# Gate chunks by twos: the seven products in another order, and a fourth place for split halves in the last pair

## The chip, the cores and the metric

The kernel runs on one core of a Trainium2 chip. The metric is the device time of one execution in microseconds (us); lower is better. Three runs of the kernel before were timed, and one further execution was profiled.

## The reference, cut to what is computed

One layer of a hybrid encoder trunk on 256 tokens of 2048 features: a mixer of two branches (retention and a gated delta rule), cross-attention, an MLP. Only the mixer's gates matter here:

```
proj = h @ w_in            # rg, gz, gate_a, gate_b are four of its parts, 2048 columns each
yr = silu(rg) * yr         # retention's output and its swish gate
yg = silu(gz) * yg         # the delta rule's output and its gate
merged = sigmoid(gate_a) * yr + sigmoid(gate_b) * yg
out = merged @ w_out
```

All data are float32. The products are computed to float32 accuracy from halves: a value is split into a rounded high half and the rest, and three matmuls (high x high, high x low, low x high) make one product.

## The kernel before

The mixer goes over four groups of columns `j` = 0 to 3, in each of which retention, the delta rule's stream and both branches' gates are computed. h1, the normalised input, stands as four quads of 512 features (each a high and a low half, 4 tiles of 128 features x 256 tokens). A gate chunk is 512 columns of `w_in`: 2048 x 512 weights in four quarters, one to a quad, of 1 MiB each. A quarter is loaded as `raw` by a DMA of SyncE's queue (SP) and split in two steps of 128 x 1024: ScalarE (ACT) copies the high half `whi` (L990), VectorE (DVE) subtracts and leaves the low half `wlo` (L991). The pool has three places for such a pair of halves, so the fourth split waits for the matmuls that read the first. A `spare` pool gives a fourth place (`whx`, `wlx`) to every fourth split; only the MLP uses it.

Retention's gate chunks of j = 1, 2, 3 and the delta rule's of j = 3 are computed by twos, in `two_chunks`. Two chunks are two columns of blocks, `n` = 0 and 1, over the quads `q`, and the two token tiles `t` of 128 are the rows. Two of the four quads are computed plainly: `plain(n, q)` is 24 matmuls (4 feature tiles x 2 token tiles x 3). For the two other quads, 2 x 2 blocks of tokens and features meet 2 x 2 blocks of weights, and seven products do the work of eight: b11, p5, b22, the second sum of x, b21, y and the fourth sum of x. A product is 12 matmuls. It needs sums of tokens (`s_in`, built once by `sums_of_tokens` when j = 1, L936) and sums of weights, x and y, each in two tiles (`xa`, `xb`, `ya`, `yb`) of 128 x 1024. A sum of weights is built by a plain load through SP's queue (`load_parts`) and an adding transfer through GpSimd's (POOL) queue (`add_parts`, L971, 512 KB each), or by an addition on VectorE (`add_to`, L977). x changes its value three times in a pair, each time by a transfer that adds to what is there, so it cannot start before the last split that reads the old value. `moved` says which sums go by transfers.

`finish` adds the kept sums (`u`, `d`) to a chunk's result and applies the gate: `gth` (L1087, L1089), then a product with `yr` or `yg`. `others(q)` is used in the last pair alone: `take_back(q)` splits a kept quad `mg` of merged results of an earlier j again, by a copy q (L1128) and a subtraction (L1129), into a quad of h1 that no one reads any more. It is the operand of `w_out`, which follows the last pair. In the retention pairs steps of the delta rule's core (`steps`, with `ro` at L274 on GpSimd, `qe` at L855 and `yg` at L858) stand between the products: `step` runs one after each product and after every four triples (12 matmuls) of a plain product.

Every engine runs its own queue in order. The order comes from the order of the program and from priorities: loads, splits and adding transfers run ahead of the matmuls that need them (`tc.high_priority`), `tc.issue_after` keeps chosen instructions of one engine in sequence, and `behind` puts work behind the latest split.

Of the kernel before, what the change touches and what calls it, by code (L numbers as in the profile page):

```python
# [10 lines left out]
F32 = mybir.dt.float32  # L11
# [6 lines left out]
P = 128  # L18
# [36 lines left out]
def trunk(ctx: ExitStack, tc: tile.TileContext, x_f, mem_f, positions, lead_f, small_f, w_blocks, w_chunks, w_ga,  # L55
# [30 lines left out]
    def half_tiles():  # L86

        turn[0] += 1
        if spare and turn[0] % 4 == 0:
            return tuple(spare[0].tile([P, 1024 + room], F32R, name=nm, tag=nm, bufs=1)  # L90
                         for nm, room in (("whx", 128), ("wlx", 0)))
        return tuple(wp.tile([P, 1024 + room], F32R, name=nm, tag=nm, bufs=3) for nm, room in (("whi", 64), ("wlo", 0)))

    @contextmanager
# [841 lines left out]
    def sums_of_tokens(i):  # L936

        xs = mx.tile([P, 2, 512], F32, name="xs", tag="qk", bufs=1)
        whole, sv = (xs[:, e, :].rearrange("p (a n) -> p a n", a=n) for e, n in ((0, 2), (1, 4)))
        for g in range(2):  # L940
            vec.tensor_add(whole[:, g], *(h1[g].both[:, i, c:c + S].bitcast(F32) for c in (0, S)))
        (a11, a21), (a12, a22) = ((whole[:, g, 0:P], whole[:, g, P:S]) for g in range(2))
        vec.tensor_sub(sv[:, 0], a21, a22)
        vec.tensor_sub(sv[:, 1], sv[:, 0], a11)
        vec.tensor_sub(sv[:, 2], a11, a21)
        vec.tensor_add(sv[:, 3], a12, sv[:, 1])
        split([a[:, i, :] for a in s_in], xs[:, 1, :])

    def two_chunks(chunks, evacs, before=None, moved=("x2", "x4", "y")):

        own = [stream_ps(), stream_ps()]
        shared, p5 = bank("c"), bank("c")
        kept_back.append(None)
        x, y = ([mx.tile([P, 1024], F32, name=n, tag=tag, bufs=1) for n, tag in these]
                for these in ((("xa", "kq"), ("xb", "lw")), (("ya", "qk"), ("yb", "tw"))))
        opened, ends = set(), []

        def lines(n, q, h):  # L960
            return w_chunks[chunks[n], q][:, h * 1024:(h + 1) * 1024]

        def load_parts(to, n, q):
            with tc.high_priority(offset=100000), tc.issue_after(fetched[-1]):
                for h in range(2):
                    fetched.append(nc.sync.dma_start(to[h], lines(n, q, h)).ins)

        def add_parts(to, n, q):
            with tc.high_priority(offset=100000):
                for h in range(2):  # L970
                    pool.dma_start(to[h], lines(n, q, h), accum_op=ALU.add)  # L971

        def add_to(to, src):
            with tc.high_priority(offset=100000):
                for h in range(2):
                    with tc.issue_after(latest["lo"]):
                        vec.tensor_add(to[h], to[h], src[h])  # L977

        def load(n, q):
            raw = wp.tile([P, 4 * 512], F32, name="raw", tag="raw", bufs=3)  # L980
            with tc.high_priority(offset=100000):
                fetched.append(nc.sync.dma_start(raw, w_chunks[chunks[n], q]).ins)
            return raw[:, 0:1024], raw[:, 1024:2048]

        def parted(srcs):
            halves = []
            with tc.high_priority(offset=100000):
                for src in srcs:
                    hi, lo = (h[:, :1024] for h in half_tiles())
                    latest["hi"] = act.activation(hi, src, AF.Copy).ins  # L990
                    latest["lo"] = vec.tensor_sub(lo, src, hi.bitcast(F32)).ins  # L991
                    halves.append([a.rearrange("p (k n) -> p k n", n=512) for a in (hi, lo)])
            return halves

        def triple(o, lhs, rhs, key):
            for l, r in ((0, 0), (0, 1), (1, 0)):
                with tc.issue_after(ends[-1]) if ends else ExitStack():
                    ins = pe.matmul(o, lhs[l], rhs[r], start=key not in opened, stop=False, skip_group_check=True).ins  # L998
                opened.add(key)
            return ins  # L1000

        def product(o, lhs, srcs, key):
            halves = parted(srcs)
            for i in range(4):
                ins = triple(o, lhs(i), [a[:, i % 2, :] for a in halves[i // 2]], key)
            ends.append(ins)
            step()

        def plain(n, q, by_rows=False):
            halves = parted(load(n, q))  # L1010
            for c, (i, t) in enumerate([(i, t) for t in range(NT) for i in range(4)] if by_rows else
                                       [(i, t) for i in range(4) for t in range(NT)]):
                ins = triple(own[n][t], [a[:, i, t * P:(t + 1) * P] for a in h1[q]],
                             [a[:, i % 2, :] for a in halves[i // 2]], (n, t))
                if c % 4 == 3:
                    ends.append(ins)
                    step()

        def part(g, t):
            return lambda i: [a[:, i, t * P:(t + 1) * P] for a in h1[g]]  # L1020

        def summed(c):
            return lambda i: [a[:, i, c * P:(c + 1) * P] for a in s_in]

        def kept_sum(tag, ps):
            o = mx.tile([P, 2, 512], F32, name="u", tag=tag, bufs=1)
            act.activation(o[:, 0], ps, AF.Copy)
            return o

        def finish(n, t, more):  # L1030
            with tc.high_priority(offset=50000):
                evacs[n](t, own[n][t], 0, 512, more)

        def others(q):
            if before:
                before(q)

        plain(0, 2)
        load_parts(x, 1, 0)
        if "x1" in moved:  # L1040
            add_parts(x, 0, 0)
        b11 = load(0, 0)
        product(shared, part(0, 0), b11, "shared")
        if "x1" not in moved:
            add_to(x, b11)
        with tc.high_priority(offset=50000):
            u = kept_sum("vh", shared)
        u1, u3 = u[:, 0], u[:, 1]
        product(p5, summed(0), x, "p5")
        add_parts(x, 1, 1)  # L1050
        plain(0, 3)
        load_parts(y, 1, 0)
        if "y" in moved:
            add_parts(y, 1, 1)
        b22 = load(1, 1)
        product(own[1][0], summed(3), b22, (1, 0))
        product(shared, summed(1), x, "shared")
        add_parts(x, 0, 1)
        if "y" not in moved:
            add_to(y, b22)  # L1060
        with tc.high_priority(offset=50000):
            d = kept_sum("vl", shared)
        others(1)
        plain(1, 2)
        b21 = load(0, 1)
        product(own[0][0], part(1, 0), b21, (0, 0))
        finish(0, 0, u1)
        product(shared, summed(2), y, "shared")
        with tc.high_priority(offset=50000):
            act.activation(u3, shared, AF.Copy)  # L1070
            vec.tensor_sub(d[:, 0], p5, d[:, 0])
            vec.tensor_sub(d[:, 1], p5, u3)
        product(own[0][1], part(1, 1), x, (0, 1))
        finish(0, 1, u3)
        others(2)
        with behind():
            others(3)
        plain(1, 3, True)
        kept_back.clear()
        for t in range(NT):  # L1080
            finish(1, t, d[:, t])

    def gates():
        def gate_of(ps, f, scale, more):
# [20 lines left out]

        def of_retention(j, yr):
            if j in (1, 2, 3):
                two_chunks((H_RG + j, H_TA + j), (silu_gate(yr), sig_gate(yr)))
                return
            chunk(h1, cols(w_chunks, H_RG + j), silu_gate(yr))  # L1110
            chunk(h1, cols(w_chunks, H_TA + j), sig_gate(yr))

        def of_delta_rule(j, yr, yg, quad, before=None):
            if j in (3,):
                two_chunks((H_GZ + j, H_TB + j), (silu_gate(yg), sig_gate(yg, yr)), before, ("x1", "x2", "x4"))
            else:
                chunk(h1, cols(w_chunks, H_GZ + j), silu_gate(yg))
                chunk(h1, cols(w_chunks, H_TB + j), sig_gate(yg, yr), before=before, cuts=2 if before else 1)
            to_feature(lambda t, f: yg[:, t, f * P:(f + 1) * P], quad)
# [434 lines left out]
    for fb in range(4):  # L1554
# [4 lines left out]
        for b2 in range(8):  # L1559
# [13 lines left out]
            blocks(h3, w_ff1, 8 * fb + b2, 2, evac_h, ends)  # L1573
            if fb == 0:
                if b2 == 0:
                    spare.append(fp)
                for b8 in ((), (0, 1, 2), (3, 4, 5), (6, 7), (), (), (), ())[b2]:
                    place(b8)
            if b2 > 2:
# [72 lines left out]
```

## Time and profile before

| | |
|---|---|
| runs | 2036.26, 2037.98, 2039.83 us; median 2037.98 |
| profiled execution: own time, span | 2036.82 us, 2035.1 us |
| granted TensorE clock, mean | 0.999 |
| TensorE busy | 2020.7 us, 99% of the span |
| VectorE, ScalarE, GpSimd busy | 1618.4 us (80%), 1239.9 us (61%), 63.2 us (3%) |
| retention's pairs | 524 to 579, 739 to 793, 953 to 1008 us |
| the delta rule's pair | 1008 to 1056 us |

TensorE is busy nearly throughout, so what the change can move is TensorE's idle time and the number of its matmuls. In the profile a tile's name is given without its number; q is any quad (h1's or one taken back), `sh` and `sl` are the halves of `s_in`, `s` and `b` are PSUM banks, L998 is the one line that issues all matmuls of the pairs. A row of a timeline has the start, the time, the engine, the line, the operation and the tile, and in brackets how long the engine sat idle before and for whom. The rest of the profile is read in the prediction.

### The profile page before, as it was taken

Reading aid. Unit: us, or ns where it says so; the run is one execution under the profiler, and the core shown is the slowest. Engines: PE = TensorE matmul, PEld = TensorE weight load, DVE = VectorE, ACT = ScalarE, POOL = GpSimd, SP = SyncE. Lnnn points to the kernel's source line nnn. Section 1 sums busy time; section 2 is a strip of 40 time slices with the busy share of each in tenths; the row PEclk is TensorE's granted clock in tenths of the full one; section 3 lists DMA queues with packets and bytes.
Section 4 is the critical chain, followed back from the end, with each engine's and each line's share of the span. In section 5 each row is a group of like instructions: output and inputs, shape, how many; then the busy total and the mean of one; then the engine's idle time right before and its main releaser. Section 6 shows DMA issues by size and latency. Waiting matters only on the chain.

```text
span 2035.1 us, 28641 instructions
## 1 busy us (share of the span) xinstructions
PE 2020.7 (99%) x10742; PEld 1741.5 (86%) x10742; DVE 1618.4 (80%) x2507; ACT 1239.9 (61%) x2029; POOL 63.2 (3%) x74
## 2 busy tenths in 40 slices
PE   9999999999999999999999999999999999999998
PEld 8888888988888888888878899888888888888886
DVE  5887788879778887888877766777887887888788
ACT  5665765675567555755655565566557556656665
POOL 0000000000100010000100000000000000000000
PEclk9999999999999999999999999999999999999999
DMA  8678556455945585557876654568546646554661
GB/s 329 206 265 293 186 184 200 158 191 188 282 166 181 193 265 184 191 180 238 253 225 232 212 182 164 175 217 277 207 135 238 215 156 220 196 205 171 237 233 62
DMA packets 84683, 422.03 MB, mean 207 GB/s; under 512 B 17072, under 2 KB 25152, under 8 KB 40256
## 3 DMA queue, kind: packets, MB, share of 16 engines
q1 hardware_dynamic: 80656, 406.93, 57.7%
q0 software_dynamic: 3456, 12.58, 3.4%
q8 instruction: 84, 1.38, 0.3%
q10 hardware_dynamic: 432, 0.69, 0.1%
q14 instruction: 55, 0.45, 0.1%
HBM read 406.52 MB, written 11.55 MB: 205 GB/s over the span
## 4 chain that ended last, share of the span: by engine, by line
PE 96%; DVE 2%; DMA 1%; issue 0%; ACT 0%; POOLq 0%; DVEq 0%; POOL 0%; ACTq 0%
PE s L218 52%; PE s L1398 7%; PE b L1398 7%; PE s L998 5%; PE s L175 5%; PE s L174 5%; PE s L176 5%; PE b L998 2%; PE s L407 1%; PE s L408 1%; PE s L409 1%; PE b L802 1%; PE b L705 1%; PE b L146 1%; PE b L835 1%; PE b L145 1%
## 5 line engine op out<-in xcount | busy, mean ns | idle before, releaser
L218 PE MATMUL s<-q,whi 128*128 128x512 f32 x2824 | 971.0, 391 | 0.0
L129 ACT ACTIVATE whi<-raw 128x1024 fp32r<-128x1024 f32 x535 | 567.7, 1061 | 420.1 <-PE s L218 222.3
L130 DVE TENSOR_TENSOR wlo<-raw,whi 128x1024 fp32r<-128x1024 f32 x535 | 652.2, 1221 | 213.3 <-ACT whi L129 209.5
L218 PE MATMUL s<-q,wlo 128*128 128x256 f32 x2824 | 765.1, 281 | 0.0
L218 PEld LDWEIGHTS s<-q,whi 128*128 128x128 f32 x2824 | 521.5, 188 | 100.6
L218 PEld LDWEIGHTS s<-q,wlo 128*128 128x128 f32 x2824 | 528.5, 188 | 13.4 <-DVE wlo L130 0.4
L175 PE MATMUL s<-wlo,q 128*128 128x512 f32 x448 | 176.3, 394 | 0.0
L176 PE MATMUL s<-whi,q 128*128 128x512 f32 x448 | 174.6, 390 | 0.0
L174 PE MATMUL s<-whi,q 128*128 128x512 f32 x448 | 159.0, 390 | 0.0
L227 ACT ACTIVATE bo<-s 128x256 f32<-128x256 f32 x192 | 73.2, 381 | 109.9 <-PE s L218 109.8
L1398 PE MATMUL s<-whi,q 128*128 128x512 f32 x384 | 122.1, 389 | 0.0
L228 DVE TENSOR_TENSOR bo<-bo,s 128x256 f32<-128x256 f32 x192 | 79.9, 416 | 40.9 <-ACT bo L227 40.4
L998 PE MATMUL s<-whi,q 128*128 128x512 f32 x320 | 101.3, 390 | 0.0
L174 PEld LDWEIGHTS s<-whi,q 128*128 128x128 f32 x448 | 84.0, 188 | 17.5
L176 PEld LDWEIGHTS s<-whi,q 128*128 128x128 f32 x448 | 84.2, 188 | 16.8
L175 PEld LDWEIGHTS s<-wlo,q 128*128 128x128 f32 x448 | 84.2, 188 | 16.5
L1421 DVE TENSOR_TENSOR wlo<-rt,whi 128x1024 fp32r<-128x1024 f32 x55 | 67.4, 1225 | 35.9 <-ACT whi L1420 35.5
L218 PE MATMUL s<-q,whx 128*128 128x512 f32 x248 | 86.6, 390 | 0.0
L1398 PEld LDWEIGHTS s<-whi,q 128*128 128x128 f32 x384 | 72.1, 188 | 15.0
L1420 ACT ACTIVATE whi<-rt 128x1024 fp32r<-128x1024 f32 x55 | 58.3, 1061 | 41.7 <-PE s L1398 29.4
L991 DVE TENSOR_TENSOR wlo<-raw,whi 128x1024 fp32r<-128x1024 f32 x56 | 68.1, 1223 | 13.6 <-ACT whi L990 13.3
L990 ACT ACTIVATE whi<-raw 128x1024 fp32r<-128x1024 f32 x56 | 59.0, 1058 | 29.5 <-PE s L998 17.8
(405 smaller groups left out, 2977.0 us busy)
## 6 DMA issues: line engine op xcount, KB each, us to landing
raw<-w_ff SPq DMA_DIRECT2D x96, 1024.0 KB
raw<-w_chunks SPq DMA_DIRECT2D x76, 1024.0 KB
raw<-w_blocks SPq DMA_DIRECT2D x64, 1024.0 KB
raw<-w_xk SPq DMA_DIRECT2D x16, 1024.0 KB
raw<-w_out SPq DMA_DIRECT2D x16, 1024.0 KB
raw<-w_xq SPq DMA_DIRECT2D x16, 1024.0 KB
raw<-w_xo SPq DMA_DIRECT2D x16, 1024.0 KB
rt<-w_ff SPq DMA_DIRECT2D x16, 1024.0 KB
```

What stands on the lines that cost most here:

```text
L129: latest["hi"] = act.activation(hi[:, cs], src[:, cs], AF.Copy).ins
L130: latest["lo"] = vec.tensor_sub(lo[:, cs], src[:, cs], hi[:, cs].bitcast(F32)).ins
L174: pe.matmul(o, xh, wh, start=first, stop=False)
L175: pe.matmul(o, xh, wl, start=False, stop=False)
L176: pe.matmul(o, xl, wh, start=False, stop=last)
L218: ins = pe.matmul(ps[b][:, :S] if part else ps[b], halves[h][part][:, i, b * P:(b + 1) * P], x[:, kk % 4, :], start=kk == 0 and not part, ...
L227: act.activation(o, ps[b][:, S:], AF.Copy)
L228: vec.tensor_add(o, o, ps[b][:, :S])
L991: latest["lo"] = vec.tensor_sub(lo, src, hi.bitcast(F32)).ins
L998: ins = pe.matmul(o, lhs[l], rhs[r], start=key not in opened, stop=False, skip_group_check=True).ins
L1398: ins = pe.matmul(o, lhs[l], rhs[r], start=key not in opened, stop=last and j == 2, skip_group_check=True).ins
L1421: latest["lo"] = vec.tensor_sub(lo, raw[:, c:c + 1024], hi.bitcast(F32)).ins
```

## The change

The two chunks of a pair change places (the sigmoid's chunk is now `n` = 0), the plain products take quads 0 and 1, the seven products quads 2 and 3, and the order is another: `plain(1, 0)` stands before the second sum of x, and the product of x's fourth sum is the last of the pair, behind the last plain product and behind `finish` of chunk 1. In the last pair there is a fourth place for halves, in the tiles "kq" and "lw" that x had; x goes to "r4" and "g_a"; y is summed by adding transfers, and `take_back` no longer waits by `behind`.

```diff
     def half_tiles():
         turn[0] += 1
         if spare and turn[0] % 4 == 0:
-            return tuple(spare[0].tile([P, 1024 + room], F32R, name=nm, tag=nm, bufs=1)
-                         for nm, room in (("whx", 128), ("wlx", 0)))
+            return spare[0]()
...
     def sums_of_tokens(i):
-            vec.tensor_add(whole[:, g], *(h1[g].both[:, i, c:c + S].bitcast(F32) for c in (0, S)))
+            vec.tensor_add(whole[:, g], *(h1[2 + g].both[:, i, c:c + S].bitcast(F32) for c in (0, S)))
...
-    def two_chunks(chunks, evacs, before=None, moved=("x2", "x4", "y")):
+    def two_chunks(chunks, evacs, before=None, moved=("x2", "x4", "y"), places=("kq", "lw")):
-        own = [stream_ps(), stream_ps()]
+        own = {1: stream_ps(), 0: stream_ps()}
...
-        plain(0, 2)
-        load_parts(x, 1, 0)
+        plain(0, 0)
+        load_parts(x, 1, 2)
         if "x1" in moved:
-            add_parts(x, 0, 0)
-        b11 = load(0, 0)
-        product(shared, part(0, 0), b11, "shared")
+            add_parts(x, 0, 2)
+        b11 = load(0, 2)
+        product(shared, part(2, 0), b11, "shared")
...
         product(p5, summed(0), x, "p5")
-        add_parts(x, 1, 1)
-        plain(0, 3)
-        load_parts(y, 1, 0)
+        add_parts(x, 1, 3)
+        plain(0, 1)
+        load_parts(y, 1, 2)
         if "y" in moved:
-            add_parts(y, 1, 1)
-        b22 = load(1, 1)
+            add_parts(y, 1, 3)
+        b22 = load(1, 3)
         product(own[1][0], summed(3), b22, (1, 0))
+        others(1)
+        plain(1, 0)
         product(shared, summed(1), x, "shared")
-        add_parts(x, 0, 1)
+        add_parts(x, 0, 3)
...
-        others(1)
-        plain(1, 2)
-        b21 = load(0, 1)
-        product(own[0][0], part(1, 0), b21, (0, 0))
-        finish(0, 0, u1)
+        others(2)
+        b21 = load(0, 3)
+        product(own[0][0], part(3, 0), b21, (0, 0))
         product(shared, summed(2), y, "shared")
...
-        product(own[0][1], part(1, 1), x, (0, 1))
-        finish(0, 1, u3)
-        others(2)
-        with behind():
-            others(3)
-        plain(1, 3, True)
-        kept_back.clear()
+        plain(1, 1, True)
+        others(3)
         for t in range(NT):
             finish(1, t, d[:, t])
+        finish(0, 0, u1)
+        product(own[0][1], part(3, 1), x, (0, 1))
+        kept_back.clear()
+        finish(0, 1, u3)
...
-                two_chunks((H_RG + j, H_TA + j), (silu_gate(yr), sig_gate(yr)))
+                two_chunks((H_TA + j, H_RG + j), (sig_gate(yr), silu_gate(yr)))
...
-                two_chunks((H_GZ + j, H_TB + j), (silu_gate(yg), sig_gate(yg, yr)), before, ("x1", "x2", "x4"))
+                spare.append(lambda: tuple(mx.tile([P, 1024], F32R, name=nm, tag=tag, bufs=1)
+                                           for nm, tag in (("whx", "kq"), ("wlx", "lw"))))
+                two_chunks((H_TB + j, H_GZ + j), (sig_gate(yg, yr), silu_gate(yg)), before, ("x1", "x2", "x4", "y"), ("r4", "g_a"))
+                spare.clear()
```

Three places show how the change moves instructions. Line numbers of the changed kernel are one or two lower.

ScalarE in the last pair, around the product p5. raw_10028 is the load of b11, raw_10074 that of the plain product behind p5, raw_10110 (raw_10112 after) that of b22, and xa_9986, xb_9987 are x. Before:

```order
L990 ACTIVATE whi_10030<-raw_10028 128x1024
L990 ACTIVATE whi_10034<-raw_10028 128x1024
L1089 ACTIVATE gth_9975<-gth_9975 128x512
L990 ACTIVATE whi_10052<-xa_9986 128x1024
L990 ACTIVATE whi_10056<-xb_9987 128x1024
L990 ACTIVATE whi_10076<-raw_10074 128x1024
L1027 ACTIVATE u_10050<-b_9984 128x512
L1128 ACTIVATE q_10268<-mg_6710 128x4x256
L990 ACTIVATE whi_10080<-raw_10074 128x1024
L990 ACTIVATE whi_10112<-raw_10110 128x1024
```

and now:

```order
L989 ACTIVATE whi_10034<-raw_10028 128x1024
L989 ACTIVATE whi_10052<-xa_9986 128x1024
L1087 ACTIVATE gth_9951<-gth_9951 128x512
L989 ACTIVATE whi_10076<-raw_10074 128x1024
L1087 ACTIVATE gth_9975<-gth_9975 128x512
L989 ACTIVATE whi_10080<-raw_10074 128x1024
L1026 ACTIVATE u_10050<-b_9984 128x512
L1129 ACTIVATE q_10195<-mg_6710 128x4x256
L989 ACTIVATE whx_10056<-xb_9987 128x1024
L989 ACTIVATE whi_10114<-raw_10112 128x1024
```

The split of `xb`, which p5 reads, stood ahead of both splits of raw_10074; now it stands behind them and behind the copies u and q.

GpSimd's queue over the beginning of the last pair. Before:

```order
L274 TENSOR_TENSOR ro_9707<-qe_9705,nhalf_pow_89 128x4
L971 DMA xa_9986<-w_chunks 128x1024
L971 DMA xb_9987<-w_chunks 128x1024
L274 TENSOR_TENSOR ro_9707<-qe_9705,nhalf_pow_89 128x4
L971 DMA xa_9986<-w_chunks 128x1024
```

and now:

```order
L273 TENSOR_TENSOR ro_9707<-qe_9705,nhalf_pow_89 128x4
L970 DMA xa_9986<-w_chunks 128x1024
L273 TENSOR_TENSOR ro_9707<-qe_9705,nhalf_pow_89 128x4
L970 DMA ya_9988<-w_chunks 128x1024
L970 DMA yb_9989<-w_chunks 128x1024
L970 DMA xb_9987<-w_chunks 128x1024
L970 DMA xa_9986<-w_chunks 128x1024
```

Two adding transfers for y are new, and the first one for `xb` went behind them and behind a step of the core.

VectorE at the end of the second retention pair; raw_7880 is the load of the work that follows the pair, and q, yg, qe, ro belong to the delta rule's core. Before:

```order
L1087 TENSOR_TENSOR gth_7828<-s1_7445,u_7546 128x512
L855 SCALAR_TENSOR_TENSOR qe_7600<-so_7601,qe4_5769 128x4
L130 TENSOR_TENSOR wlo_7883<-raw_7880,whi_7882 128x1024
L1095 SCALAR_TENSOR_TENSOR yr_7013<-gth_7828,yr_7013 128x512
L858 SCALAR_TENSOR_TENSOR yg_7014<-b_7698,ro_7602,small_111 128x128 x4
L1087 TENSOR_TENSOR gth_7866<-s0_7446,u_7723 128x512
L130 TENSOR_TENSOR wlo_7887<-raw_7880,whi_7886 128x1024
```

and now:

```order
L1085 TENSOR_TENSOR gth_7838<-s0_7444,u_7757 128x512
L854 SCALAR_TENSOR_TENSOR qe_7600<-so_7601,qe4_5769 128x4
L1093 SCALAR_TENSOR_TENSOR yr_7013<-gth_7838,yr_7013 128x512
L857 SCALAR_TENSOR_TENSOR yg_7014<-b_7700,ro_7602,small_111 128x128 x4
L990 TENSOR_TENSOR wlo_7855<-xb_7451,whi_7854 128x1024
L1085 TENSOR_TENSOR gth_7842<-s1_7445,u_7757 128x512
L129 TENSOR_TENSOR wlo_7883<-raw_7880,whi_7882 128x1024
L129 TENSOR_TENSOR wlo_7887<-raw_7880,whi_7886 128x1024
```

The last product of the pair needs wlo_7855; its subtraction now stands behind the gate and the core's normalisation, and both subtractions of the following load stand behind it.

More of the change, by code (lines that the diff above doesn't have):

```diff
@@ L947, in sums_of_tokens @@
         split([a[:, i, :] for a in s_in], xs[:, 1, :])
-    def two_chunks(chunks, evacs, before=None, moved=("x2", "x4", "y")):
-        own = [stream_ps(), stream_ps()]
+    def two_chunks(chunks, evacs, before=None, moved=("x2", "x4", "y"), places=("kq", "lw")):
+        own = {1: stream_ps(), 0: stream_ps()}
         shared, p5 = bank("c"), bank("c")
         kept_back.append(None)
-        x, y = ([mx.tile([P, 1024], F32, name=n, tag=tag, bufs=1) for n, tag in these]
-                for these in ((("xa", "kq"), ("xb", "lw")), (("ya", "qk"), ("yb", "tw"))))
+        x, y = ([mx.tile([P, 1024], F32, name=n + e, tag=tag, bufs=1) for e, tag in zip("ab", tags)]
+                for n, tags in (("x", places), ("y", ("qk", "tw"))))
         opened, ends = set(), []
@@ L1575, in trunk @@
                 if b2 == 0:
-                    spare.append(fp)
+                    spare.append(lambda: tuple(fp.tile([P, 1024 + room], F32R, name=nm, tag=nm, bufs=1)
+                                               for nm, room in (("whx", 128), ("wlx", 0))))
                 for b8 in ((), (0, 1, 2), (3, 4, 5), (6, 7), (), (), (), ())[b2]:
```

## Prediction

> **What bounds the kernel now.** I read the page's busy shares first, then the waits of TensorE, then a table of the four stretches in which pairs of gate chunks are computed, and last, instruction by instruction, the places where TensorE stood still. The page's engine line and the whole list of TensorE's waits:
>
> ```profile
> PE 2020.7 (99%) x10742; PEld 1741.5 (86%) x10742; DVE 1618.4 (80%) x2507; ACT 1239.9 (61%) x2029; POOL 63.2 (3%) x74
> PE s L998 <- DVE wlo L991: 2.7, 3, 1.5
> PE b L266 <- DVE warm L262: 1.1, 1, 1.1
> PE s L407 <- DVE q L343: 1.1, 1, 1.1
> PE b L998 <- DVE wlo L991: 0.4, 1, 0.4
> ```
>
> TensorE is the bound for 99% of the span. Only the rows of L998, the matmuls of the pairs, touch what is changed; they add up to 3.1 us in four waits, each for a low half `wlo` that VectorE subtracts. Which pair has them shows in the stretches (after the colon: length; then busy time and instructions of PE, weight loads, VectorE, ScalarE, GpSimd; granted clock, DMA share, GB/s):
>
> ```profile
> 524.00:579.00 55.00, 55.00 (x294) 47.10 (x293) 45.98 (x73) 36.36 (x61) 10.76 (x12) 1.00 0.76 215
> 953.00:1008.00 55.00, 55.00 (x292) 47.06 (x291) 45.93 (x73) 35.26 (x59) 11.44 (x12) 1.00 0.86 243
> 1008.00:1056.00 48.00, 44.84 (x198) 35.61 (x197) 39.22 (x40) 29.98 (x34) 3.46 (x4) 1.00 0.74 235
> ```
>
> In the first and third retention pairs (the second, not shown, is alike) TensorE is busy in the whole stretch: a rearrangement there has nothing to win. All four waits lie in the last stretch, the delta rule's pair. TensorE's timeline at them, and the chain of waits ahead of the first two:
>
> ```profile
> 1028.02 0.50 PE L998 MATMUL b<-wlo,sh 128*128 128x512 f32 x1 [0.44 <-DVE wlo L991]
> 1029.29 0.61 PE L998 MATMUL s<-whi,q 128*128 128x512 f32 x2
> 1031.43 0.50 PE L998 MATMUL s<-wlo,q 128*128 128x512 f32 x1 [1.52 <-DVE wlo L991]
> 1031.76 0.40 PE L998 MATMUL s<-whi,q 128*128 128x512 f32 x1
> 1046.25 0.50 PE L998 MATMUL s<-wlo,q 128*128 128x512 f32 x1 [1.00 <-DVE wlo L991]
> 1048.58 0.50 PE L998 MATMUL s<-wlo,q 128*128 128x512 f32 x1 [0.20 <-DVE wlo L991]
> 1016.25 9.29 DMA xb<-w_chunks
> 1029.02 1.22 DVE yb L977
> 1030.24 1.15 DVE wlo L991
> 571.13 6.60 PE s L998 x29
> ```
>
> The last row, 29 matmuls of the first pair in 6.60 us, gives the pace: 0.2276 us each. At 1029.29 two matmuls start that should need 0.46 us; the next starts 2.14 us later, so the 1.52 us wait costs 1.68 us, and the restarted matmul holds its successor 0.33 instead of 0.23 us, 0.11 more. Each wait therefore costs 0.27 us beyond what is listed: 0.44 + 1.52 + 1.00 + 0.20 + 4 x 0.27 = **4.2 us, the most that this change can win**. It is 0.21% of the time; what a measurement of this kernel can tell from no change is about 0.2%, 4.1 us.
>
> **Part 1, the four stalls: -4.2 us.** The first two come of x's second sum. Its adding transfers cannot be issued before the last reader of x's old value is done, 1014.83 for `xa` and
>
> ```profile
> 1016.25 0.86 POOL L971 DMA_DIRECT2D xb<-w_chunks  x1 [0.54 <-DVE wlo L991]
> ```
>
> for `xb`, and `xb` lands 9.29 us later, at 1025.54, while TensorE reaches the product that reads it at 24 + 12 matmuls (8.2 us) after p5. Then ScalarE's and VectorE's splits come late, and two plain additions (L977, y's sum, 1.22 us for `yb`) stand ahead of the next `wlo`. After the change a plain product of 24 matmuls moves ahead: 60 matmuls, 13.65 us, where issue to landing and two splits (1.06 and 1.23 us) take some 12 us; and y is summed by transfers, so those additions leave VectorE. The other two stalls (1046, 1048) come of `wlo` queued on VectorE behind take_back's subtraction and the gates' work; the product before the end now has its operand at least 48 matmuls after it is asked for, and the last plain product stands ahead of take_back's last part. I walked the rest of the new order on the five engines with these durations and found no other late operand. All four go.
>
> **Part 2, a new wait at p5, last pair: +3.8 us.** In the new order ScalarE splits p5's second half (`whx` from `xb`) behind three rows that need b11's end: the second split of the plain product after p5 (it takes the place that b11's second half has left), the copy u, and take_back's copy q. Before, the `xb` split stood ahead of all of them. The same rows, in the old order:
>
> ```profile
> 1014.94 1.06 ACT L990 ACTIVATE whi<-raw 128x1024 fp32r<-128x1024 f32 x1 [0.25 <-PE b L998]
> 1015.91 0.58 ACT L1027 ACTIVATE u<-b 128x512 f32<-128x512 f32 x1
> 1016.38 1.05 ACT L1128 ACTIVATE q<-mg 128x1024 fp32r<-128x1024 f32 x1
> 1017.33 2.00 ACT L990 ACTIVATE whi<-raw 128x1024 fp32r<-128x1024 f32 x2
> 1017.47 1.23 DVE L1129 TENSOR_TENSOR q<-mg,q 128x1024 fp32r<-128x1024 f32 x1 [0.21 <-ACT q L1128]
> 1018.61 2.35 DVE L991 TENSOR_TENSOR wlo<-raw,whi 128x1024 fp32r<-128x1024 f32 x2
> 1014.74 0.39 PE L998 MATMUL b<-whi,sh 128*128 128x512 f32 x1
> ```
>
> They start 0.97, 0.47 and 0.95 us apart, so `whx` starts 2.39 us after the first of them. VectorE subtracts for it behind q's subtraction: 1018.61 is 3.67 us after 1014.94, and 1.23 us more makes 4.90. With 0.20 us from TensorE's last b11 matmul to ScalarE (1014.74 to 1014.94) and 0.04 us back (the subtraction of 1030.24 ends at 1031.39, TensorE starts at 1031.43), p5's eighth matmul can start 5.14 us after b11's end. By pace it would start after 7 x 0.2276 = 1.59 us. That is 3.55 us, and 0.22 for two restarts (the seventh waits for `whx`, the eighth for its low half): +3.8 us. It lies wholly on TensorE, whose queue is in order; nothing covers it. The bounds: zero, if b11's end and the earlier split leave room that I don't see, and 5.2 us, if another 1.2 us subtraction slips in.
>
> **Part 3, the end of each retention pair: +1.3 us in three.** The pair used to end with a plain product; now it ends with the product of x's fourth sum, 12 matmuls, directly behind finish of the other chunk. At the end of the first pair before:
>
> ```profile
> 572.32 0.69 DVE L1087 TENSOR_TENSOR gth<-s,u 128x512 f32<-128x512 f32 x1
> 572.93 0.16 DVE L855 SCALAR_TENSOR_TENSOR qe<-so,qe 128x4 f32<-128x4 f32 x1
> 573.16 1.01 POOL L274 TENSOR_TENSOR ro<-qe,nhalf_pow 128x4 f32<-128x4 f32 x1 [7.03 <-DVE qe L855]
> 573.72 1.23 DVE L130 TENSOR_TENSOR wlo<-raw,whi 128x1024 fp32r<-128x1024 f32 x1 [0.64 <-ACT whi L129]
> 575.46 1.12 DVE L858 SCALAR_TENSOR_TENSOR yg<-b,ro,small 128x128 f32<-128x128 f32 x4
> 576.50 0.68 DVE L1087 TENSOR_TENSOR gth<-s,u 128x512 f32<-128x512 f32 x1
> 577.37 0.61 ACT L1089 ACTIVATE gth<-gth 128x512 f32<-128x512 f32 x1
> ```
>
> After the change VectorE's queue after the last plain product reads: gth, qe, yr, yg x4, then the subtraction for x's second half, gth, the subtraction for the load that follows the pair. From the plain product's end: gth starts after 0.25 (as ScalarE did at 1014.94), qe 0.61 later; 0.23 to GpSimd and 1.01 there, in whose shade yr runs, and 0.15 back by estimate make 2.25; yg's four take 1.04 to the next start (575.46 to 576.50), 3.29; the subtraction 1.22, 4.51. TensorE asks for it after 20 matmuls, 4.55 us: no wait. By VectorE's spacing of starts (1.14 after a subtraction, 0.61 after a gth) the following subtraction runs from 5.04 to 6.26. TensorE asks after 26 matmuls, 5.92 us: 0.34 late, with a restart 0.45 us, three times 1.3 us. Bounds: none, and 0.45 + 1.2 us each (one more subtraction in the way), 5 us in all.
>
> **Part 4, at nothing.** Two more adding transfers in the last pair, and two additions fewer on VectorE (2 x 1.22 us, off the path after part 1). The DMA rows of 1000 to 1056 us:
>
> ```profile
> q1 hardware_dynamic: 1559, 9.86, 45.3%
> q0 software_dynamic: 864, 3.15, 30.8%
> xb<-w_chunks POOLq DMA_DIRECT2D x3, 512.0 KB, 9.3
> yb<-w_chunks POOLq DMA_DIRECT2D x1, 512.0 KB, 11.6
> ```
>
> 3.15 MB in 30.8% of 56 us are six transfers of 2.87 us each; two more take 5.7 us. The last stretch's DMA share of 0.74 in 48 us leaves 12.5 us. The last row is from the third retention pair and is the longest landing that I found. What is nearest to an edge is x's first sum in the last pair: `xb`'s addition is now behind ro, `ya` and `yb` in GpSimd's queue, because its load waits for a place (`g_a`) that the delta rule's core holds until some 6.6 us before b11's end. Three transfers of 2.87 us from 3 us before that end, and 2.6 us from data to landing, give 8.2 us after it on a clock that ScalarE reads at 11.2: 3 us of cover. Issues to GpSimd's queue cost it about 0.9 us each, with VectorE 80% busy beside them. [...] The issue row of 1016.25, 0.86 us beside a subtraction, shows no lengthening.
>
> The sum: -4.2 + 3.8 + 1.3 = **+0.9 us**. The profiled execution took 2036.82 us, so 2037.7; the median of the runs, 2037.98, is 1.16 above it, so **2038.9 us**.
>
> **The rivals.**
> (a) The stalls go and nothing new comes: -4.2, 2033.8. For it: TensorE's queue could find `whx` early if the row ahead of it on ScalarE waited less. Against it: the three rows need b11's end, in both orders.
> (b) Slower: plain(1, 0) now stands before the product that it followed, so in the retention pairs its load is wanted 12 matmuls, 2.73 us, earlier. In the third pair:
>
> ```profile
> 971.32 4.45 SPq L982 DMA_DIRECT2D raw<-w_chunks  x2
> GB/s 453 360 415 328 202 180 191 120 153 169 246 191 317 366 404 382 219 202 202 202 202 213 202 350 415 377 229 229 284 415 393 229 191 213 208 186 213 202 257 295
> 978.32 0.39 PE L998 MATMUL b<-whi,sh 128*128 128x512 f32 x1
> ```
>
> The load of 971.32 is the burst near 400 GB/s in the slices (0.75 us each from 956) that end near 976.2; two splits make 978.6. In the new order its low half is read at 978.32 + 0.46 = 978.8: 0.2 us of cover. It decides from 1.1 us late in each of three pairs (0.9 + 3.3 = 4.2); 2 us late gives +6.9, 2044.9. Against it: a plain load is issued when a raw buffer comes free, and that moves forward too.
> (c) The adding transfer of part 4 outlasts its cover: it lands 11.6 us after issue, or worse, and p5 waits up to 4 us: 2040 to 2043.
> (d) The change does not do what it says: the second sum stays late as before, and the new waits add: +5.1, 2043.
>
> **How the numbers follow.** My forecast 0.68, own range 2036 to 2041.5 from the bounds of parts 2 and 3; (a) 0.08; (b) 0.12; (c) 0.08; (d) 0.04. Faster by over 0.2% needs nearly all of (a): 0.09 with a hundredth of the forecast. Slower: three quarters of (b), half of (c), all of (d): 0.17. Same: the rest, 0.74. The range leaves out some of each end: 2034.5 to 2043.0.
>
> **What would show it.** Part 1: no wait at the two products after p5 nor in the last plain product. Part 2: in the last pair a wait of 2 to 4 us of TensorE for ScalarE's `whx` and VectorE's `wlx` in p5's second half. Part 3: 0.1 to 0.5 us waits for `wlo` at the load after each retention pair. Rival (b) shows as a wait for a `raw` transfer at plain(1, 0). If p5 shows no wait, part 2 is wrong and the time is near 2035.

## The result, and the profile after

The changed kernel took 2047.59 us (median of six runs, 2045.92 to 2047.95) against 2038.62 us for the kernel before (six runs, 2036.26 to 2040.44): slower, ratio 1.0042 with a 95% interval of 1.0031 to 1.0053. The prediction, 2038.9 us with a range to 2043.0, was too low by 8.7 us. The profiled execution took 2047.52 us. Three runs in the sets below took 2505 to 6397 us (one of the kernel before, one of the last pair alone, one of the version that turns out fastest) and are left out of the medians.

The engine line of the page and, out of TensorE's waits, those in lines of the change:

```profile
PE 2024.2 (99%) x10742; PEld 1743.3 (85%) x10742; DVE 1614.6 (79%) x2505; ACT 1240.5 (61%) x2029; POOL 64.5 (3%) x76
PE b L997 <- ACT whx L989: 9.1, 1, 9.1
PE b L997 <- DVE wlx L990: 0.5, 1, 0.5
PE s L217 <- DVE wlo L129: 0.2, 1, 0.2
```

The four old waits for `wlo` in the last pair are gone. In their place stands one of 9.1 us: p5's second half waits for `whx`. TensorE's timeline there, and a table by stretch (length; busy time of PE, weight loads, VectorE, ScalarE, GpSimd; granted clock, DMA share, GB/s):

```profile
1017.97 0.40 PE L997 MATMUL b<-whi,sl 128*128 128x512 f32 x1
1027.44 0.79 PE L997 MATMUL b<-whx,sh 128*128 128x512 f32 x1 [9.07 <-ACT whx L989]
1028.70 0.79 PE L997 MATMUL b<-wlx,sh 128*128 128x512 f32 x1 [0.47 <-DVE wlx L990]
...
1033.97 0.39 PE L997 MATMUL s<-wlo,q 128*128 128x512 f32 x1
1008.00:1066.00 58.00, 48.39 (x202) 38.60 (x201) 38.65 (x39) 28.92 (x33) 5.22 (x7) 0.88 0.77 218
1020.50:1033.50 13.00, 5.59 (x12) 4.08 (x13) 3.88 (x4) 3.06 (x3) 0.86 (x1) 0.50 0.87 215
1034.00:1038.00 4.00, 4.00 (x19) 3.31 (x18) 1.23 (x1) 1.06 (x1) 0.00 (x0) 1.00 0.80 263
```

The matmul due at 1018.20 starts at 1027.44, 9.24 us late. Then a second loss shows: the granted clock is 0.50 from 1020.3 to 1033.9, and the 13 matmuls from 1027.44 on need 6.53 us to 1033.97 where 13 x 0.2276 = 2.96 is the pace. All in all 15.77 us for 2.96: **12.8 us lost**, of which 9.2 by the late operand, 1.0 at its low half and 2.5 by the clock behind that (the slow clock has a part of the 1.0 too).

Why `whx` is late is in the chain of waits; the second fence has SP's and GpSimd's queues, the third what ScalarE and VectorE did meanwhile:

```profile
1001.74 10.90 DMA xb<-w_chunks
...
1013.20 13.11 DMA xb<-w_chunks
1026.31 0.02 issue
1026.33 1.06 ACT whx L989
```

```profile
999.42 0.33 SPq L981 DMA_DIRECT2D raw<-w_chunks  x1
999.80 0.42 SPq L965 DMA_DIRECT2D ya<-w_chunks  x1
1000.27 0.42 SPq L965 DMA_DIRECT2D yb<-w_chunks  x1
1001.74 0.33 SPq L965 DMA_DIRECT2D xb<-w_chunks  x1
1007.22 0.90 POOL L970 DMA_DIRECT2D ya<-w_chunks  x1 [2.49 <-DMA ya<-w_chunks]
1011.33 0.85 POOL L970 DMA_DIRECT2D yb<-w_chunks  x1 [3.21 <-DMA yb<-w_chunks]
1013.20 0.86 POOL L970 DMA_DIRECT2D xb<-w_chunks  x1 [1.03 <-DMA xb<-w_chunks]
```

```profile
1018.55 1.04 ACT L1129 ACTIVATE q<-mg 128x1024 fp32r<-128x1024 f32 x1
1026.33 1.06 ACT L989 ACTIVATE whx<-xb 128x1024 fp32r<-128x1024 f32 x1 [6.74 <-DMA xb<-w_chunks]
1019.62 1.22 DVE L1130 TENSOR_TENSOR q<-mg,q 128x1024 fp32r<-128x1024 f32 x1
```

xb's plain load runs behind a 1 MiB load and y's two loads: 10.9 us, though 512 KB is 1.35 us of all engines by the plain queue's row in the prediction (9.86 MB in 45.3% of 56 us). Its adding transfer can only then be issued, behind y's, and lands 13.1 us later. ScalarE was free for it from 1019.6 on. The DMA engines over 1011.0 to 1026.3 us (packets, MB, share of the 16 engines):

```profile
q0 software_dynamic: 480, 1.77, 58.1%
q1 hardware_dynamic: 394, 2.84, 46.2%
```

They are full, and the adding transfers (q0) have little more than half of them; the rest goes to plain loads of later work (q1). By the landings behind their issues (8.4, 10.1 and 13.1 us), `ya`, `yb` and `xb` land at 1015.6, 1021.4 and 1026.3: one every 5 to 6 us, where the prediction counted 2.87 each.

### The profile page after: what moved, and what is told of

Same layout as the page of the kernel before. It is cut to its first block, busy times and chain, and to the rows that moved or that the text cites. A ratio compares the mean times of both kernels' runs of the same rounds, so it can differ in the third digit from the quotient of the medians.

```text
span 2045.6 us, 28648 instructions
## 1 busy us (share of the span) xinstructions
PE 2024.2 (99%) x10742; PEld 1743.3 (85%) x10742; DVE 1614.6 (79%) x2505; ACT 1240.5 (61%) x2029; POOL 64.5 (3%) x76
## 4 chain that ended last, share of the span: by engine, by line
PE 94%; DVE 3%; DMA 2%; issue 1%; ACT 1%; POOLq 0%; SPq 0%; DVEq 0%; POOL 0%; ACTq 0%
PE s L217 51%; PE s L1399 7%; PE b L1399 7%; PE s L174 5%; PE s L175 5%; PE s L173 5%; PE s L997 5%; PE b L997 2%; DMA xb<-w_chunks 1%; PE s L406 1%; PE s L407 1%; PE s L408 1%; PE b L801 1%; DVE wlo L129 1%; PE b L145 1%
## 5 line engine op out<-in xcount | busy, mean ns | idle before, releaser
L174 PEld LDWEIGHTS s<-wlo,q 128*128 128x128 f32 x448 | 84.2, 188 | 16.6
```

The source lines that it names most:

```text
L174: pe.matmul(o, xh, wl, start=False, stop=False)
```

## The experiments

Theory A, in the form that it had from the fifth run on: x's first sum is late because its load begins late, in a place that comes free late, and because y's transfers run beside and ahead of it. (In the first four runs it named y's loads and transfers alone.) Rivals: B, retention's new order pushes the last pair's beginning together, whatever y does; C, ScalarE's order around p5 (part 2 of the prediction) is a cost of its own; D, the DMA engines have too little left in this stretch in any order. In the runs where the kernel before ran beside the others it took 2037.79, 2037.99 and 2037.98 us (medians of 25 to 32 runs).

**Three parts undone one at a time, and one constraint.** y by VectorE again:

```diff
-two_chunks(..., before, ("x1", "x2", "x4", "y"), ("r4", "g_a"))
+two_chunks(..., before, ("x1", "x2", "x4"), ("r4", "g_a"))
```

> The changed kernel, but y of the last pair is summed by VectorE again: its two adding transfers are gone, its loads still stand ahead of xb's load on SP's queue. Theory A (x's first sum is late because its load stands behind y's loads and its adding transfer behind y's two): xb lands near 1018 to 1019 instead of 1026.3, TensorE's wait in p5 falls from 9.1 us to 0 to 3 us, the half clock after it goes; about 2035 to 2038 us. Rival B (retention's new order pushes the last pair together, the two transfers are a minor part): the wait stays above 6 us, 2044 or more. Rival C (ScalarE's order around p5, my part 2, is a cost of its own): 3.6 us of wait stay, 2038.4.

2041.54 us, 1.0014 (1.0005 to 1.0022): 6 us better than the change, yet slower than before. xb is added behind no transfer of y and still waits for its load until 1010.86:

```profile
1021.09 0.79 PE L997 MATMUL b<-whx,sh 128*128 128x512 f32 x1 [4.25 <-ACT whx L989]
```

Between A's and B's numbers: y's adding transfers were worth more than half of the stall, and something else the rest.

The new order in the last pair alone:

```diff
 def of_retention(j, yr):
-    two_chunks((H_TA + j, H_RG + j), (sig_gate(yr), silu_gate(yr)))
+    two_chunks_old((H_RG + j, H_TA + j), (silu_gate(yr), sig_gate(yr)))
```

> The new order in the last pair alone, with its fourth place and y's adding transfers; retention's three pairs in the old order of products (on the renamed quads). On SP's queue xa and xb are then loaded ahead of ya and yb, on GpSimd's xb is added ahead of y. Theory A: x is in time though all the transfers are there; no stall in p5, the four old stalls gone, no waits after retention's pairs: 2038.6 - 4.2 = 2034.4 us. Rival D (the DMA engines are too full in this stretch whatever the order): p5 waits 3 us or more, 2038 to 2044. Rival C: 3.6 us at p5, 2038.

2039.21 us, 1.0007 (0.9998 to 1.0016). xb is loaded ahead of y here, and p5 waits only 0.8 us, for `wlx`, but waits at x's second product have come: 1.6 and 0.8 us in its first half, 2.3 and 0.8 us in its second.

```profile
PE b L997 <- ACT whx L989: 2.3, 1, 2.3
PE b L997 <- ACT whi L989: 1.6, 1, 1.6
PE b L997 <- DVE wlx L990: 1.5, 2, 0.8
```

The 2034.4 us of A did not come, though x's first sum was in time but for 0.8 us: the second adding transfer of xb, issued at 1017.65 behind y's two, took 20.1 us to land. D looks right here.

The new order in retention's pairs alone, x in the change's places:

```diff
-two_chunks((H_TB + j, H_GZ + j), ..., ("x1", "x2", "x4", "y"), ("r4", "g_a"))
+two_chunks_old((H_GZ + j, H_TB + j), ..., ("x1", "x2", "x4"), ("r4", "g_a"))
```

> The new order in retention's three pairs alone; the last pair in the old order, three places, y by VectorE, x in the tiles r4 and g_a (its old tiles are held to the end of the third retention pair now). Part 3 of the prediction: waits for wlo at the load after each retention pair, 0.3 to 0.45 us each, +1.0 to +1.3 us. xb's load stands behind y's loads here too, without y's adding transfers. Theory A: x's first sum at most 0 to 3 us late, the old stalls remain: 2039.6 to 2042.6. Rival B: a stall of 6 us or more in p5: 2045 or more.

2042.48 us, 1.0022 (1.0012 to 1.0032). p5 waits 3.4 us for `whi` of xb, then 0.5, and the old stalls (2.4 us in three) are there as well. The time lies in A's range, the wait a little above A's 3 us; the 6 us of B did not come. So the late first sum of x needs neither the last pair's new order nor y's adding transfers: retention's order and x's new places are enough for a part of it.

The change with y's loads and adding transfers issued behind x's first:

```diff
+with tc.issue_after(loaded[1]):   # y's loads behind xb's load
     fetched.append(nc.sync.dma_start(to[h], lines(n, q, h)).ins)
...
+with tc.issue_after(added[1]):    # y's adding transfers behind xb's first
     pool.dma_start(to[h], lines(n, q, h), accum_op=ALU.add)
```

> The changed kernel with one constraint: y's loads and adding transfers are issued behind x's first ones. All transfers stay. Theory A: xb's load runs at once, its adding transfer lands near 1014 to 1016, no wait of TensorE in p5, clock 1.00 throughout, only the 1.0 us after retention's pairs left: 2034.5 to 2036 us, faster than before. Rival D (too many bytes for the time): xb or then y late by 3 us or more: 2038 to 2044.

2040.06 us, 1.0009 (1.0000 to 1.0018): 7.5 us better than the change, but again not faster than before. A's landing near 1014 to 1016 did not come, and the time is in D's range. xb is now ahead of y in both queues, and its adding transfer still took long; it lands at 1021.8, and in the profiled execution, the slowest of the eleven (2043.67 us), p5 waits 5.2 us:

```profile
1001.15 8.05 DMA xb<-w_chunks
...
1009.76 12.07 DMA xb<-w_chunks
```

In these 12 us the plain queue had 59.6% of the engines and the adding one 38.7%, which `xb` shared with `ya` and `yb` close behind it: q0 moved 0.83 MB in them, and `xb` is 0.52. Being first helps, but what follows closely takes engine time too. So the transfers have to begin early or be fewer.

**Beginning early: x back in its old tiles.** With retention's old order, kq and lw are free early, and x can be loaded first:

```diff
-spare: whx in "kq", wlx in "lw"; x in ("r4", "g_a"); moved = ("x1", "x2", "x4", "y")
+spare: whx in "r4", wlx in "g_a"; x in ("kq", "lw"); moved = ("x1", "x2", "x4")
+retention: two_chunks_old
```

> Retention's pairs in the old order; the last pair in the new order with x in its old tiles kq and lw (free early, so xa and xb are loaded first), the fourth place in r4 and g_a, and y summed by VectorE: no transfer more than before. Theory A (x's first sum is late by its place and by the transfers beside it): p5 waits for nothing, the second sum has its 60 matmuls, all four old stalls go: 2037.8 - 4.2 = 2033.6 us, between 2033 and 2035. Rival D (DMA engines too full whatever is done): a wait of 2 us or more at p5 or at x's second product, 2036 or more.

**2032.55 us, 0.9972 (0.9962 to 0.9982): faster than both kernels.** (The expectations below say 2033.1; the profiled execution took 2033.13.) I call it the fast version. TensorE has no wait left in any pair; the other two rows are ScalarE's split of xb for p5 and take_back's copy:

```profile
1008.00:1056.00 48.00, 48.00 (x221) 39.58 (x220) 40.71 (x42) 30.27 (x35) 3.45 (x4) 1.00 0.80 256
1013.43 1.06 ACT L989 ACTIVATE whx<-xb 128x1024 fp32r<-128x1024 f32 x1 [1.29 <-DMA xb<-w_chunks]
1016.77 1.05 ACT L1263 ACTIVATE q<-mg 128x1024 fp32r<-128x1024 f32 x1
```

This is part 1 of the prediction by itself: -4.2 was the sum, 5.4 was measured, with an interval of 3.7 to 7.7 us. Part 2's wait is absent because xb's split stands ahead of the copies u and q here, not behind them as in the changed kernel. And y's two additions are still on VectorE: the stalls went by the order of products, without the additions' leaving, on which part 1 also counted. One thing blurs the size of the gain. Of the 25 runs of the kernel before in this set, seven had a mean granted clock of 0.997 and took 2040.7 us in the median, and fifteen had 0.999 and took 2037.6; the fast version had 0.998 or 0.999 in all eight. So a part of the 5.4 us may be half clock that follows the old stalls in some executions. That is not shown: the kept trace of before has a clock of 1.00 in the pairs.

The same, with y by adding transfers:

> The same with y summed by adding transfers, the only difference. Theory A: they find room, 2033 to 2035 us. Rival D: as in the run with the new order in the last pair alone, where x's second xb landed 20 us after its issue, the two transfers push x's second sum past its 60 matmuls: waits of 1.5 to 4 us there, 2035.5 to 2038.

2040.93 us, 1.0014 (1.0005 to 1.0023): these two transfers cost 8.4 us, more than either number expected. Four adding transfers are issued within 2.4 us (`ya` 1013.05, `yb` 1014.33, `xa` 1014.87, `xb` 1015.45) and land 8.8, 12.5, 17.0 and 20.8 us after their issues, at 1021.9, 1026.8, 1031.9 and 1036.2, in the order of their issue and 4.3 to 5.0 us apart:

```profile
1015.45 20.77 DMA xb<-w_chunks
PE b L997 <- ACT whi L989: 3.3, 1, 3.3
```

Over 1015.5 to 1036 us the adding transfers (q0) had 51.3% of the 16 DMA engines and the plain loads (q1) 42.5%, 94% together.

Without the fourth place:

```diff
-spare.append(...)
```

> As the first of these, but without the fourth place: the order of products alone. The stalls at x's second sum (first two of the old four, 2.3 us with restarts) go by the order; the stalls behind take_back at the end (1.5 us) may stay without a fourth place: 2033.6 to 2035.5 us.

2033.55 us, 0.9977 (0.9968 to 0.9986), with one wait of 0.6 us. The gain comes of the order of products; the fourth place adds 1.0 us between the medians, about what the one wait and its restart cost, but the intervals overlap.

**The clock.** 38 matmuls that nobody reads, in the stall of the changed kernel:

```diff
 product(p5, ...):  between the halves
+for k in range(38):
+    pe.matmul(idle, h1[0][0][:, 0, :P], halves[0][0][:, 0, :], ...)
```

> The changed kernel with 38 matmuls that nobody reads (38 x 0.2276 = 8.6 us) put into TensorE's idle time in p5, between its halves. The late xb stays as it is. If the half clock after the stall comes of TensorE's idleness, the clock stays at 1.00 and the 13 matmuls after the stall take 0.23 instead of 0.43 us: 3.0 us less than the changed kernel, 2043.5 to 2045. If the clock falls for another reason, 2047.

2044.79 us, 1.0032 (1.0019 to 1.0044), 2.8 less than the change's median, and the clock stays at 1.00 where the changed kernel had 0.50 from 1020.3 to 1033.9, as the starts 0.23 to 0.24 us apart behind the last wait show:

```profile
1028.82 0.50 PE L997 MATMUL b<-wlx,sh 128*128 128x512 f32 x1 [0.68 <-DVE wlx L990]
1029.15 0.39 PE L997 MATMUL b<-whx,sl 128*128 128x512 f32 x1
1029.39 0.40 PE L997 MATMUL b<-whx,sh 128*128 128x512 f32 x1
1028.00:1033.00 5.00, 4.32 (x19) 3.46 (x19) 3.22 (x3) 2.06 (x2) 0.86 (x1) 1.00 0.70 137
```

The half clock of this stall comes of TensorE's idleness, and is a price of its own. (The medians are of two sessions and their intervals overlap; the matmul's 0.23 us instead of 0.43 does not hang on that.)

**ScalarE's order, the queue's order, the kind of transfer, the place.** take_back's copy forced ahead of xb's split in the fast version:

```diff
+others(1)
+others(2)                                  # both ahead of product(p5, ...)
+with tc.issue_after(latest["q"]):          # whx <- xb behind the copy q
     latest["hi"] = act.activation(hi, src, AF.Copy).ins
```

> The fast version (new order in the last pair alone, x in kq and lw, y by VectorE; 2033.1 us), with take_back's copy q forced ahead of the split of xb on ScalarE, as in the changed kernel (there a second split and the copy u stand ahead too). xb is in time here, so this is part 2 of the prediction by itself: q starts 0.2 us after b11's end, the split of xb 0.95 later, its subtraction behind q's ends 3.6 us after b11's end where TensorE asks at 1.6: a wait of 2.1 us and two restarts, 2035.4 us. If part 2 is wrong, no wait and 2033.1.

2035.74 us, 0.9986 (0.9978 to 0.9995), 3.2 more than the fast version:

```profile
1015.62 0.40 PE L999 MATMUL b<-whi,sl 128*128 128x512 f32 x1
1016.71 0.50 PE L999 MATMUL b<-whx,sh 128*128 128x512 f32 x1 [0.69 <-ACT whx L990]
1018.16 0.50 PE L999 MATMUL b<-wlx,sh 128*128 128x512 f32 x1 [0.95 <-DVE wlx L992]
1018.50 0.39 PE L999 MATMUL b<-whx,sl 128*128 128x512 f32 x1
1020.00:1022.00 2.00, 2.00 (x7) 1.52 (x6) 1.60 (x2) 0.73 (x1) 0.00 (x0) 0.50 0.99 184
```

From 1015.62 to 1018.50 are 2.88 us for three starts that should take 0.69: 2.2 us are lost, as part 2's way of counting gives (2.3): C is shown. What it leaves out is the half clock, which came even here and costs another 1.6 us in this trace: the eight matmuls from 1019.43 on take 3.40 us where 1.82 is the pace.

y's adding transfers behind x's second pair, all bytes as in the version of 2040.93 us:

```diff
+with tc.issue_after(added[3]):
     pool.dma_start(y, ..., accum_op=ALU.add)
```

> The version with y by adding transfers that took 2040.9 us, with one constraint: y's two adding transfers are issued behind x's second pair, not ahead. The same bytes. Queue theory (adding transfers are served one behind another, 4 to 5 us each while plain loads run beside them): x's second xb lands about 10 us after its issue instead of 20.8, before TensorE asks; y lands about 10 us later, still in time: no wait, 2033 to 2034.5. Rival D (the engines' capacity): the waits move to y's product, 2036 to 2041.

2034.26 us, 0.9980 (0.9971 to 0.9989). Now y lands last, 16.6 and 20.6 us after its issues, and its product waits 1.9 us: it needs a PSUM bank that the copy u empties, and u stands behind the split of `yb` in ScalarE's queue:

```profile
1015.45 20.58 DMA yb<-w_chunks
PE b L998 <- ACT u L1027: 1.9, 1, 1.9
```

The same transfers, in the order in which they are wanted, cost 1.7 us instead of 8.4. Rival D falls as the reason of the 8.4: the order in the queue decides.

y's two transfers without their addition:

```diff
-pool.dma_start(y, ..., accum_op=ALU.add)
+pool.dma_start(y, ...)
```

> The same version of 2040.9 us, in which y's two transfers through GpSimd's queue are plain ones: the addition is left out, the bytes and the order stay. If what counts is that adding is slow (2.87 us of all engines for 512 KB against 1.35): x's second xb lands some 5 to 6 us earlier, at 1030 to 1031, and the waits nearly go: 2033 to 2035. If the queue's order or the bytes alone count: 2038 to 2041.

2037.33 us, 0.9994 (0.9985 to 1.0003), between the two numbers. The second xb lands 16.91 us after its issue instead of 20.77: 3.9 of the expected 5 to 6 us come of the addition, and two plain transfers ahead in the queue delay it enough to leave waits of 1.6 and 0.8 us.

The fast version with x and the fourth place exchanged:

> The fast version with the places exchanged as the change has them: x in r4 and g_a, the fourth place in kq and lw. Only the time at which xb's load can start differs (g_a is free about 1.2 us later than lw was). If the place by itself costs: xb's first sum is 1 to 2 us late, 2034 to 2036; if it needs the other transfers to matter: no wait, 2033 to 2034.

2036.83 us, 0.9993 (0.9984 to 1.0001), 4.3 more than the fast version and a little above the 2034 to 2036 expected: p5 waits 1.5 and 0.8 us. xb's load starts at 1000.28 instead of 998.71, its adding transfer at 1006.22 instead of 1002.81, and the clock halves behind the wait (0.50 from 1020.2 to 1023.6):

```profile
1000.28 0.33 SPq L965 DMA_DIRECT2D xb<-w_chunks  x1
1006.22 0.86 POOL L970 DMA_DIRECT2D xb<-w_chunks  x1 [5.57 <-PE s L1130]
1018.11 0.50 PE L997 MATMUL b<-whx,sh 128*128 128x512 f32 x1 [1.51 <-ACT whx L989]
```

The place by itself costs. A load that begins 1.6 us later comes with an adding transfer that begins 3.4 us later. (The profile puts the wait ahead of that transfer down to a matmul. The load is the likelier reason: in the run of the last pair alone, with the same places, the transfer begins 5.4 us behind its load and the profile names the load.)

**What the runs add up to.** From the fast version, 2032.55 us: the places, +4.3; y's transfers on top (the run of the last pair alone, 2039.2), +2.4; retention's new order on top (the change, 2047.6), +8.4. Of the last step 1.3 us are the waits behind retention's pairs. For the rest of it rival B has a part: with x in r4 and g_a and y by VectorE, retention's order alone makes 2036.83 into 2041.54, since ya and yb are then loaded ahead of xb (its load took 10.1 us, against 5.9 or less to the issue of the next). What y's transfers cost depends on the rest: 2.4, 6.0 and 8.4 us in three settings. (The kernel before, which ran in every set, differs by 0.2 us between the sets of the experiments and by up to 0.8 us from that of the change, 2038.62.) How the DMA engines share themselves out among the loads in flight was not tried beyond this.

## Why the prediction was wrong, step by step

- **Part 1 (-4.2): right.** None of the four stalls is in the changed kernel. That alone would prove little, since every later operand had 12.8 us more time there; but the fast version, which has none of the other costs, won 5.4 us with no wait left.
- **Part 2 (+3.8): the mechanism was right, and hidden.** In the changed kernel q ends at 1019.6 and VectorE is through with it at 1020.8, so `wlx` would have been done near 1022.0, 3.6 us after the start due at 1018.43; but xb landed at 1026.3. The run with q forced ahead shows it by itself; the versions with x in time escape it because xb's split stands ahead of u and q in them.
- **Part 3 (+1.3): right.** At the first pair's end:

```profile
578.19 0.39 PE L997 MATMUL s<-whi,q 128*128 128x512 f32 x1
578.41 0.40 PE L217 MATMUL s<-q,whi 128*128 128x512 f32 x1
578.89 0.50 PE L217 MATMUL s<-q,wlo 128*128 128x256 f32 x2
```

0.48 us between starts where 0.23 is the pace, 0.10 at the restart and 0.07 at the product's own `wlo` (577.20 to 577.49) make 0.42, forecast 0.45 (1.3 for three); the second pair shows the same rows 215 us later, and at the third's end starts that are 0.24, 0.10 and 0.08 us late make the same 0.42. The 0.15 us back from GpSimd, an estimate there, was at most that: ro ends at 574.70 and yg starts at 574.85.

- **Part 4 (at nothing, "3 us of cover"): this step failed, by 9 us** (12.8 us at p5, where part 2 had 3.8). The sentence puts its clock on b11's end; its times were counted from the pair's beginning, 8.2 us earlier (1008.6 after the change: g_a's last reader ended at 1001.7, 6.9 before; ScalarE came to xb's split at 1019.6, 11 after). Read from b11's end it even contradicts part 2, which has that split 2.6 us after it. On its own clock the landing was forecast for 1016.8 and came at 1026.3. 2.87 us is what an adding transfer takes of all 16 engines, and I set three of them end to end, from 3 us before the pair's beginning, as if nothing else ran. `ya` was to land at 1011.1 (1005.6 + 2.87 + 2.6) and landed at 1015.6: 1.6 us because its load and so its issue came late (1007.22), 2.9 because it took 8.4 us from issue to landing and not 5.5. `xb` landed 10.7 us after it, where two transfers at 2.87 make 5.7: the other 5.0 of the 9.5 us. The trace of before had the right sizes. 2.87 + 2.6 is its shortest landing, that of x's last sum (5.4 and 5.5 us); x's first sum, in the very stretch in question, took 7.9 us (`xa`) and 10.8 us (`xb`) and landed 5.7 us apart. The same counting with these figures gives 1005.6 + 7.9 + 2 x 5.7 = 1024.9, 5 us behind ScalarE. "12.5 us left" was a mean over 48 us; ahead of p5 there was nothing left, before the change either: over 1002.7 to 1012 us its trace has 55.6% of the engines for adding transfers and 41.4% for plain loads. Issues on GpSimd's queue cost what was counted for them: 0.84 to 0.90 us in the changed kernel's last pair, 0.85 to 0.91 before.
- **The clock was no term of the sum.** The trace of before shows 1.00 throughout the pairs, with no wait over 1.52 us. Every term for a new wait ought to have carried what the clock may add behind it: 2.5 to 3 us here.
- Of the rivals, (c) was the right mechanism, with a price of at most 4 us, where 12.8 were measured, and a chance of 0.08. (b), late loads in retention's pairs, did not happen.

The sum with what was measured: -4.2 + 12.8 + 1.3 = +9.9; the runs say +9.0 (6.3 to 10.8).

## What to carry to other kernels

A transfer that shares the DMA engines with prefetches is priced by the interval at which such transfers land in a full stretch (here 4.3 to 5.8 us), not by its share of the engines' time (2.87); before two are added to a queue, list what stands behind them and when each is wanted, and issue them in that order. A moved buffer moves the start of the load into it, and with it everything queued behind (with x in r4 the load began 1.6 us later, its adding transfer 3.4). And a wait of some microseconds on the engine that bounds the kernel costs more than its length when its clock falls (here 9.2 us of wait and 2.5 us of clock).

## What the hardware showed that I had not expected

The half clock lasted about 3.4 us or a multiple of that: 13.7 us in the changed kernel, 6.8 in the run with y by VectorE (1019.9 to 1026.7), 3.4 with x in r4 (1020.2 to 1023.6). The length of the waits alone did not decide whether it came: two waits of 0.69 and 0.95 us (q forced ahead) brought a piece of half clock, where one of 1.93 us (y behind x's second pair) brought none:

```profile
1036.00:1038.00 2.00, 0.27 (x1) 0.27 (x2) 0.77 (x1) 1.86 (x3) 0.00 (x0) 1.00 1.06 320
1038.00:1040.00 2.00, 2.00 (x10) 1.58 (x10) 2.00 (x3) 1.58 (x2) 0.00 (x0) 1.00 1.03 324
```

In the first case the half clock runs from 1019.4 to 1022.8, and TensorE was idle for 1.64 of the 3.4 us ahead of it. In the second it was idle for 1.93 us and the clock stayed at 1.00 (1034 to 1044). How much idleness is enough, and within what time, was not measured.
